# A mixture-of-experts loop: dispatch products moved behind the bias products, combine split into two passes inside the next pair

## The chip, the cores and the metric

The program runs on one core of one Trainium2 chip. The metric is the device time of one execution in microseconds (us); the median of three runs of the kernel before is 2145.57 us (2145.54 to 2147.9). A core has TensorE (matrix products; PE in the profile, its weight loads PEld), VectorE (DVE), ScalarE (ACT), GpSimd (POOL) and SyncE (SP), which issues the transfers from HBM here, carried out by 16 DMA engines.

## The reference

A small network on 256 tokens of width 1024: two mixing layers with cross attention and feed-forward, and then one block with a hybrid mixer and a mixture of experts. Only the last part, the experts, is touched by the change:

```python
logits = ht @ w_router + b_router
top_val, top_idx = lax.top_k(logits, 4)          # 32 experts, 4 for each token
gates = jax.nn.softmax(top_val, axis=-1)
...
hg = xblk @ w_gu[e] + b_gu[e]                    # 1024 x 2048, float32
x_glu, x_lin = hg[:, :1024], hg[:, 1024:]
act = min(x_glu, 7) * sigmoid(1.702 * min(x_glu, 7)) * (clip(x_lin, -7, 7) + 1)
y = act @ w_down[e] + b_down[e]                  # 1024 x 1024, float32
out[token] += gate * y
```

All weights are float32 and each is used once: an expert has (1024 x 2048 + 1024 x 1024) x 4 bytes = 12.6 MB, the 32 experts 403 MB.

## The kernel before

Experts are worked in 16 pairs (numbered 0 to 15 here, `moe`, L2107). A pair shares one tile of 128 token slots: pair 0 has 64 slots for each expert; the other pairs, ordered by load, have 96 for a busy expert and 32 for a light one. For each pair the program makes:

1. **dispatch** (`dispatch`, L2115): VectorE builds a selection matrix `Dm` (L2121, in a tile of the pool `sl`), TensorE multiplies the token rows by it (`dx`, 16 products of 128x128), and `modulate` (L2006) scales and shifts the result into `xg` on ScalarE and VectorE. There is one `xg`, so this comes when the pair before has read it.
2. **gate and up** (`gu`): for each k of 8, 16 products of 512 columns. A product of a 32-slot part uses a 32-column strip of TensorE's array, and four parts lie beside each other; three strips belong to the busy expert, one to the light one. Each needs its expert's 1 MB weight tile for this k. Then the bias products (L2194, bfloat16).
3. **swiglu** (L2313): on VectorE, ScalarE, VectorE, VectorE, in tiles `sg` and `sl`, two of each; then transposes on TensorE (`at`, L2209) and a copy to `ya` (L2210).
4. **down** (`dn`, L2223): 64 products of 512 columns with eight 1 MB tiles of weights.
5. **gate matrix**: VectorE builds `gw` (L2232), TensorE transposes it, ScalarE copies it to `GT` (L2235).
6. **combine** (`cb`, L2250): four float32 products of 512 columns scatter the pair's `y` to token rows; VectorE adds them to `acc` (L2251).

In the source the next pair's dispatch stands behind down (`DP = 2`). The order on each engine is written by the tile framework's scheduler, from its own estimate of when operands are ready; so in pairs 1 to 5 the 16 `dx` products follow the last `dn` product, and in later pairs they lie between `dn` products. Each engine works its queue in order.

Weights go through a ring of buffers of 22 MB, in 1 MB tiles (L1908 to L1936): the pools `blk` and `fb`, and six tiles `ringp` taken in turn (`ringt`, L1953). SP issues a transfer when the buffer's last reader is done. In pair 6 `overflow_table` (L2323) also takes one tile from `ringt`, as scratch for VectorE.

The last pair is different: `last_down` (L2254) works down in three column blocks, each followed by its combine, and the closing norm.

Of the kernel before, what the change touches and what calls it, by code (L numbers as in the profile page):

```python
# [47 lines left out]
SGB, SLB = 2, 2  # L48
# [14 lines left out]
D = 1024  # L63
T = 256
DFF = 2752
NFB = 22
NE = 32
# [158 lines left out]
class Net:  # L226
# [1880 lines left out]
    def moe(self):  # L2107


        nc = self.nc  # L2110
# [1 line left out]
        Wg, Wd = self.dr["w_gu_2"][0], self.dr["w_down_2"][0]  # L2112
        xg, pre = self.xg, self.pre

        def dispatch(pos, es, caps, first=False):  # L2115

            offs = (0, caps[0])
            Dm = self.mt2("sl", [128, 512], bufs=SLB)[:, 0:256].rearrange("p (t s) -> p t s", t=2)
            for tt in range(2):
                for i in range(2):  # L2120
                    nc.vector.tensor_scalar(Dm[:, tt, offs[i]:offs[i] + caps[i]], slot[:, 0:caps[i]], pos[:, tt, es[i]:es[i] + 1],  # L2121
                                            self.rs[:, tt:tt + 1], op0=OP.is_equal, op1=OP.mult)

            nb = 4 if first else 2
            w = 8 // nb
            dps = [self.ps("dx").rearrange("p (k t) -> p k t", k=4) for _ in range(nb)]
            for db, tt in [(db, tt) for tt in range(2) for db in range(8)] if first else [(db, tt) for db in range(8) for tt in range(2)]:

                self.mm(dps[db // w][:, db % w, :], self.x[tt][:, db * 128:db * 128 + 128], Dm[:, tt, :],
                        start=(tt == 0 and (not first or db % w == 0)), stop=(tt == 1))  # L2130
                if db % w == w - 1 and tt == 1:
                    self.modulate(xg, dps[db // w], db // w, w)

        for pair in range(NE // 2):
            first, last = pair == 0, pair == NE // 2 - 1
            if first:
                gate, pos = self.gate, self.posm
# [19 lines left out]
            def wd(i, u):  # L2157
                if first:
                    return Wd[e[i], 256 * u:256 * u + 256, :].rearrange("(a p) c -> p a c", p=128)
                if last and u < 2:  # L2160
                    return Wd[bass.ds(e[i], 1), 512 * u:512 * u + 512, 0:512].rearrange("b (a p) c -> p (b a) c", p=128)
                if last:
                    return Wd[bass.ds(e[i], 1), :, 256 * u:256 * u + 256].rearrange("b (a p) c -> p (b a) c", p=128)
                return Wd[bass.ds(e[i], 1), 256 * u:256 * u + 256, :].rearrange("b (a p) c -> p (b a) c", p=128)

            if first:
                dispatch(pos, es, caps, True)
# [24 lines left out]
            for n in range(4):  # L2192
                for o, m, i in parts:
                    self.mm(pg[n][o:o + m], sel[0:96, es[i]:es[i] + 1].to_broadcast([96, m]),  # L2194
                            self.b3[0:96, 512 * n:512 * n + 512], start=False)
            nxt = lambda at: dispatch(self.posp, (2 + pair, NE - 1 - pair), (96, 32)) if at == DP and pair < NE // 2 - 1 else None
            nxt(0)
            if last:

                self.pa = [self.ps("cb")[:, 0:256] for _ in range(2)]  # L2200
                for tt in range(2):
                    self.mm(self.pa[tt], self.ident, self.acc[tt][:, 768:1024], stop=False)
                self.warm("last")
            aT = self.ya().rearrange("p (k s) -> p k s", k=8)
            for n in range(2):
                act = self.swiglu(pg[n], pg[n + 2])
                pt = self.ps("at").rearrange("p (f s) -> p f s", f=4)
                for f in range(4):
                    nc.tensor.transpose(pt[:, f, :], act[:, 128 * f:128 * f + 128], self.ident)  # L2209
                nc.scalar.mul(aT[:, 4 * n:4 * n + 4, :], pt, 1.0 / 1.702)  # L2210
            nxt(1)
            pd = [self.ps("dn") for _ in range(2)] if not last else None
            if last:
                ws = [self.ring_pair([wd(i, u) for i in range(2)]) for u in range(4)]
            else:
                ws = [[self.ring(wd(i, u)) for i in range(2)] for u in range(4)]
            for u, w in enumerate(ws if not last else ()):
                for a in range(2):
                    k = 2 * u + a
                    for n in range(2):  # L2220
                        for o, m, i in parts:
                            c0 = a * 1024 + 512 * n
                            self.mm(pd[n][o:o + m], aT[:, k, o:o + m], w[i](c0), start=(k == 0), stop=(k == 7))  # L2223
            nxt(2)

            pgt = self.ps("gw")
            for tt in range(2):
                gw = self.mt2("gw", [128, 192])[:, 0:128]
                for i in range(2):
                    q = slice(es[i], es[i] + 1)  # L2230
                    with self.later():
                        nc.vector.tensor_scalar(gw[:, offs[i]:offs[i] + caps[i]], slot[:, 0:caps[i]], pos[:, tt, q], gate[:, tt, q], op0=OP.is_equal, op1=OP.mult)  # L2232
                nc.tensor.transpose(pgt[:, tt * 128:tt * 128 + 128], gw, self.ident)
            GT = self.mt2("GT", [128, T])
            nc.scalar.copy(GT, pgt[:, 0:T])  # L2235
            if pair == 6:
                self.overflow_table()
            elif pair == 8:
                self.overflow_slots()
            if last:  # L2240
                self.last_down(ws, aT, parts, GT)
                break
# [3 lines left out]
            for tt in range(2):  # L2246
# [76 lines left out]
    def overflow_table(self):  # L2323
# [4 lines left out]
        with self.tc.issue_after(self.last_ring.ins):  # L2328
# [15 lines left out]
        nc.vector.tensor_tensor(oh, rk.unsqueeze(1).to_broadcast([32, 16, 96]),  # L2344
                                self.C2("iota16")[0:32].unsqueeze(2).to_broadcast([32, 16, 96]), op=OP.is_equal)
        eb = self.mt("ovid", [32, 3, 16])
        for x, row in enumerate((e3, self.C2("off")[0:32], self.C2("rid")[0:32])):
            nc.vector.tensor_tensor(t2, oh, row.unsqueeze(1).to_broadcast([32, 16, 96]), op=OP.mult)
            nc.vector.tensor_reduce(eb[:, x, :], t2, axis=AX.X, op=OP.add)
# [184 lines left out]
```

## Time and profile before

| | us |
|---|---|
| median of three runs | 2145.57 |
| the profiled execution | 2153.04 |
| its span, first to last instruction | 2150.9 |
| pairs of experts, from the first gate-and-up product of pair 0 | from 1149.8 to 2150.9 |

The profiled execution is one of the kernel before, 2.1 us longer than the span that its instructions cover, and 7.5 us above the median. Over the whole span TensorE is busy 94%, VectorE 44%, ScalarE 31%. That share mixes a first half with moderate traffic from HBM and the experts' half, in which about 410 GB/s are moved. A busy TensorE need not be a TensorE at its peak: the end of a product is modelled. A float32 product has two records in the trace, so `dn` has x128 for its 64 products, `dx` x32, and `cb` x8. So the stretches are read one by one, by the windows, the timeline and the waits of SP.

### The profile page before, as it was taken

To read this page: it belongs to the slowest core of one execution; us is meant where nothing else is said; L and a number is where in the kernel's file an instruction comes from. 1 tells how busy PE (TensorE), PEld (TensorE's weight loads), DVE (VectorE), ACT (ScalarE), POOL (GpSimd) and SP (SyncE) were. 2 spreads that over 40 slices of the span, in tenths; PEclk is the share of its full clock that TensorE was granted. 3 is DMA by queue.
4 is the path that set the end of the run, shared out by engine and by line. 5 is a ranking of instruction groups with operands and counts; after the bars stand their busy time and mean duration, and the time that the engine had idled before them with its cause. 6 is when DMAs were issued, how large, how long until landed. Compare 5 with 4: busy or idle time off the path is not lost.

```text
span 2150.9 us, 37883 instructions
## 1 busy us (share of the span) xinstructions
PE 2015.1 (94%) x15056; PEld 1286.3 (60%) x15056; DVE 937.9 (44%) x1854; ACT 670.9 (31%) x1331; POOL 74.7 (3%) x97
## 2 busy tenths in 40 slices
PE   7999999999997899998989999999999999999997
PEld 6876798999985789997874333333233333333332
DVE  6764655777766457778554111111141111111122
ACT  6523554555654355555333100000000100000011
POOL 1200000000000000002001000000000000000000
PEclk9999999999998899999989999999999999999999
DMA  7459454666634546665858999999899999999992
GB/s 210 147 190 289 126 171 128 192 190 181 184 108 118 166 137 187 182 187 159 310 193 298 376 412 412 412 412 412 359 354 409 409 410 409 410 411 411 407 386 91
DMA packets 327765, 589.14 MB, mean 274 GB/s; under 512 B 25778, under 2 KB 216626, under 8 KB 318242
## 3 DMA queue, kind: packets, MB, share of 16 engines
q1 hardware_dynamic: 327586, 586.70, 76.7%
q8 instruction: 119, 1.95, 0.4%
q14 instruction: 60, 0.49, 0.1%
HBM read 585.58 MB, written 1.05 MB: 273 GB/s over the span
## 4 chain that ended last, share of the span: by engine, by line
PE 87%; DVE 4%; ACT 2%; issue 1%; DMA 1%; POOL 1%; ACTq 0%; SPq 0%; DVEq 0%; POOLq 0%
PE gu L362 22%; PE dn L362 13%; PE ug L362 11%; PE acc L362 9%; PE pj L362 6%; PE mk L362 4%; PE cb L362 3%; PE dx L362 3%; PE qp L362 2%; PE ada L362 1%; PE po L362 1%; PE tm L362 1%; PE accd L362 1%; PE at L2209 1%; DMA raw<-in_w_ada_dram 1%
## 5 line engine op out<-in xcount | busy, mean ns | idle before, releaser
L388 DVE TENSOR_TENSOR lo<-raw,hi 128x512 fp32r<-128x512 f32 x578 | 378.7, 695 | 162.2 <-ACT hi L387 146.8
L387 ACT CAST hi<-raw 128x512 fp32r<-128x512 f32 x578 | 328.7, 618 | 325.4 <-issue 85.0
L362 PE MATMUL gu<-Bring,xg 128*32 128x512 f32 (+1 forms) x3000 | 373.0, 594 | 0.0
L362 PEld LDWEIGHTS gu<-Bring,xg 128*32 128x32 f32 (+1 forms) x3000 | 110.9, 111 | 239.1 <-issue 219.3
L362 PE MATMUL dn<-Bring,ya 128*32 128x512 f32 (+2 forms) x1688 | 231.3, 599 | 1.3
L2317 DVE TENSOR_SCALAR sg<-gu 128x512 f32<-128x512 f32 x32 | 20.6, 686 | 433.1 <-PE gu L362 433.1
L362 PE MATMUL ug<-Bxh,hi 128*128 128x256 f32 x688 | 193.9, 282 | 1.4 <-ACT Bxh L487 1.4
L362 PE MATMUL ug<-Bxl,hi 128*128 128x256 f32 x688 | 193.7, 282 | 0.3 <-DVE Bxl L488 0.3
L362 PE MATMUL ug<-Bxh,lo 128*128 128x256 f32 x688 | 193.6, 282 | 0.0
L2318 ACT ACTIVATE sg<-sg 128x512 f32<-128x512 f32 x32 | 19.7, 629 | 506.6 <-DVE sg L2317 506.6
L362 PE MATMUL gu<-ring,xg 128*32 128x512 f32 (+1 forms) x968 | 174.2, 596 | 0.0
L362 PE MATMUL pj<-Bxh,hi 128*128 128x256 f32 x472 | 140.4, 298 | 8.6 <-ACT hi L387 4.1
L362 PE MATMUL pj<-Bxh,lo 128*128 128x256 f32 x472 | 138.0, 294 | 2.4 <-DVE lo L388 2.4
L362 PE MATMUL pj<-Bxl,hi 128*128 128x256 f32 x472 | 137.4, 292 | 0.9 <-DVE Bxl L488 0.6
L362 PEld LDWEIGHTS dn<-Bring,ya 128*32 128x32 f32 (+1 forms) x1688 | 60.7, 113 | 125.7 <-issue 112.5
L362 PEld LDWEIGHTS ug<-Bxh,hi 128*128 128x128 f32 x688 | 129.8, 189 | 3.9 <-ACT Bxh L487 1.8
L362 PEld LDWEIGHTS ug<-Bxl,hi 128*128 128x128 f32 x688 | 130.2, 189 | 1.9 <-DVE Bxl L488 0.5
L362 PEld LDWEIGHTS ug<-Bxh,lo 128*128 128x128 f32 x688 | 130.1, 189 | 0.0
L362 PEld LDWEIGHTS pj<-Bxh,hi 128*128 128x128 f32 x472 | 93.0, 197 | 13.5 <-ACT hi L387 5.3
L362 PEld LDWEIGHTS pj<-Bxh,lo 128*128 128x128 f32 x472 | 92.5, 196 | 5.2 <-DVE lo L388 3.0
L362 PEld LDWEIGHTS pj<-Bxl,hi 128*128 128x128 f32 x472 | 92.9, 197 | 3.8 <-issue 1.8
L362 PEld LDWEIGHTS gu<-ring,xg 128*32 128x32 f32 (+1 forms) x968 | 47.3, 111 | 75.9 <-issue 73.4
(725 smaller groups left out, 3141.5 us busy)
## 6 DMA issues: line engine op xcount, KB each, us to landing
Bring<-in_w_gu_dram SPq DMA_DIRECT2D x366, 512.0 KB, 10.2
Bring<-in_w_down_dram SPq DMA_DIRECT2D x198, 512.0 KB, 10.8
ring<-in_w_gu_dram SPq DMA_DIRECT2D x73, 1024.0 KB, 12.5
raw<-in_ffn_w_up_dram SPq DMA_DIRECT2D x84, 512.0 KB, 4.2
ring<-in_w_down_dram SPq DMA_DIRECT2D x29, 1024.0 KB, 13.3
raw<-in_w_ada_dram SPq DMA_DIRECT2D x48, 512.0 KB, 5.0
raw<-in_ffn_w_down_dram SPq DMA_DIRECT2D x42, 512.0 KB, 3.6
raw<-in_xattn_wkv_dram SPq DMA_DIRECT2D x32, 512.0 KB, 4.0
```

Of the source, the lines that this page charges most:

```text
L362: return self.nc.tensor.matmul(out, lhsT, rhs, start=start, stop=stop, skip_group_check=True)
L387: nc.scalar.copy(hi[:, s], raw[:, s])
L388: nc.vector.tensor_tensor(lo[:, s], raw[:, s], hi[:, s].bitcast(F32), op=OP.subtract)
L2209: nc.tensor.transpose(pt[:, f, :], act[:, 128 * f:128 * f + 128], self.ident)
L2317: nc.vector.tensor_scalar(g, pglu, 7.0, None, op0=OP.min)
L2318: nc.scalar.activation(g, g, AF.Silu, scale=1.702)
```

## The change

The parts of the diff that matter; the function `selection` is the first half of the old `dispatch`.

```diff
-DP = 2
+CB = 1
...
-        def dispatch(pos, es, caps, first=False):
+        def selection(pos, es, caps):
             offs = (0, caps[0])
             Dm = self.mt2("sl", [128, 512], bufs=SLB)[:, 0:256].rearrange("p (t s) -> p t s", t=2)
...
+            return Dm
+
+        def dispatch(Dm, first=False):
...
+        pending = None
...
                             self.mm(pg[n][o:o + m], xg[:, k, o:o + m], w[i](512 * n), start=(k == 0), stop=False)
+                if k == CB and pending:
+                    pending()
...
-                nc.tensor.transpose(pgt[:, tt * 128:tt * 128 + 128], gw, self.ident)
-            GT = self.mt2("GT", [128, T])
-            nc.scalar.copy(GT, pgt[:, 0:T])
+                with self.tc.issue_after(biased.ins):
+                    nc.tensor.transpose(pgt[:, tt * 128:tt * 128 + 128], gw, self.ident)
...
+                GT, gs = self.mt2("GT", [128, T], F32R), self.mt2("gs", [128, 1])
+                nc.vector.tensor_scalar(GT, pgt[:, 0:T], 0.0, None, op0=OP.is_gt)
+                nc.scalar.activation(self.mt2("gw", [128, 192]).bitcast(BF16)[:, 0:T], pgt[:, 0:T], AF.Identity, accum_out=gs)
+                with self.later():
+                    Dm = selection(self.posp, (2 + pair, NE - 1 - pair), (96, 32))
+            acts = [self.swiglu(pg[n], pg[n + 2]) for n in range(2)]
+            if not last:
+
+                with self.tc.issue_after(biased.ins):
+                    dispatch(Dm)
...
-            y = self.ya()
-            nc.scalar.copy(y[:, 0:512], pd[0])
-            nc.vector.tensor_copy(y[:, 512:1024], pd[1])
-            for tt in range(2):
+
+            yh, yl = self.mt2("ya", [128, D], F32R, bufs=1), []
+            for n in range(2):
+                h, t = yh[:, 512 * n:512 * n + 512], self.mt2("sl", [128, 512], F32R, bufs=SLB)
+                nc.scalar.mul(h, pd[n], gs)
+                nc.vector.scalar_tensor_tensor(t, pd[n], gs, h.bitcast(F32), op0=OP.mult, op1=OP.subtract)
+                yl.append(t)
+
+            def pending(GT=GT, yh=yh, yl=yl):
                 for n in range(2):
                     s = slice(512 * n, 512 * n + 512)
-                    p = self.ps("cb")
-                    self.mm(p, GT[:, tt * 128:tt * 128 + 128], y[:, s])
-                    nc.vector.tensor_tensor(self.acc[tt][:, s], p, self.acc[tt][:, s], op=OP.add)
-            nxt(3)
+                    for tt in range(2):
+                        p = self.ps("cb")
+                        g = GT[:, tt * 128:tt * 128 + 128]
+                        self.mm(p, g, yh[:, s], stop=False)
+                        self.mm(p, g, yl[n], start=False)
+                        nc.vector.tensor_tensor(self.acc[tt][:, s], p, self.acc[tt][:, s], op=OP.add)
...
-        oh, t2 = (t[0:32, 0:1536].rearrange("p (a b) -> p a b", a=16)
-                  for t in self.ringt().bitcast(BF16).rearrange("p (x c) -> x p c", x=2))
...
+        oh, t2 = (self.mt2("sg", [128, 512], bufs=SGB).bitcast(BF16)[0:32, 0:768].rearrange("p (a b) -> p a b", a=8) for _ in range(2))
+        for b in (slice(0, 8), slice(8, 16)):
```

In words: the dispatch products of the next pair and the two transposes of the gate matrix now stand behind the bias products, while swiglu runs. `GT` becomes a matrix of zeros and ones, the gate of each slot a column `gs`; down's result is multiplied by `gs` when it leaves PSUM, as a high part (ScalarE) and the rest (VectorE), both in the format `fp32r` that TensorE multiplies in one pass. The combine has two such products in place of each float32 one, and is written behind the gate-and-up products of k = 1 of the next pair. The table of pair 6 uses two `sg` tiles, in two halves, in place of a ring tile. Pair 15 keeps its gate matrix, float32 combine and `last_down`. SP's order of weight transfers is the same in both kernels.

TensorE's queue behind the bias products of pair 4 (`b` bias, `sel3p` selector) in the kernel before:

```order
L362 MATMUL gu_13626<-b_12166,sel3p 32x512
L2209 MATMUL at_13830<-c_70,sg_13824 128x128 x4
L2209 MATMUL at_13842<-c_70,sg_13836 128x128 x4
L362 MATMUL dn_13848<-Bring_13850,ya_13823 32x512 x3
...
L362 MATMUL dn_13849<-Bring_13879,ya_13823 32x512
L362 MATMUL dx_13951<-sl_13946,h_66 128x128
L362 MATMUL dx_13951<-sl_13946,h_68 128x128
```

And in the kernel after, at the same place:

```order
L362 MATMUL gu_13654<-b_12166,sel3p 32x512
L2212 MATMUL gw_13867<-c_70,gw_13868 128x128
L2212 MATMUL gw_13867<-c_70,gw_13872 128x128
L362 MATMUL dx_13898<-sl_13881,h_66 128x128
L362 MATMUL dx_13898<-sl_13881,h_68 128x128
...
L2237 MATMUL at_13925<-c_70,sg_13886 128x128 x4
L2237 MATMUL at_13931<-c_70,sg_13892 128x128 x4
L362 MATMUL dn_13937<-Bring_13939,ya_13924 32x512 x3
```

The two gate transposes and all 16 dispatch products (`dx`) moved from behind `dn` to ahead of the swiglu transposes (`at`).

TensorE's queue near the start of pair 9's gate and up (k = 1; `x3` the busy expert's three strips, the single rows the light expert's) in the kernel before:

```order
L362 MATMUL gu_15666<-Bring_15694,xg 32x512 x3
L362 MATMUL gu_15667<-Bring_15694,xg 32x512 x3
L362 MATMUL gu_15668<-Bring_15695,xg 32x512 x3
L362 MATMUL gu_15669<-Bring_15695,xg 32x512 x3
L362 MATMUL gu_15666<-ring_15698,xg 32x512
L362 MATMUL gu_15667<-ring_15698,xg 32x512
L362 MATMUL gu_15668<-ring_15698,xg 32x512
L362 MATMUL gu_15669<-ring_15698,xg 32x512
```

And in the kernel after (k = 0), where the combine of pair 8 stands between the two experts' products of one k:

```order
L362 MATMUL gu_15759<-Bring_15762,xg 32x512 x3
L362 MATMUL gu_15760<-Bring_15762,xg 32x512 x3
L362 MATMUL cb_15807<-ya_15730,GT_15555 128x512
L362 MATMUL cb_15811<-ya_15730,GT_15555 128x512
L362 MATMUL cb_15807<-sl_15731,GT_15555 128x512
L362 MATMUL cb_15811<-sl_15731,GT_15555 128x512
...
L362 MATMUL gu_15757<-Bring_15765,xg 32x512
L362 MATMUL gu_15758<-Bring_15765,xg 32x512
```

The eight `cb` products moved into the next pair, behind the busy expert's products of its first k; in both kernels the light expert's four follow the other's twelve, in the kernel after from pair 4 on and in part of pair 3, before from pair 7 on.

VectorE's queue in swiglu of pair 5 in the kernel after:

```order
L2337 TENSOR_SCALAR sg_14297<-gu_14062 128x512
L2337 TENSOR_SCALAR sg_14303<-gu_14063 128x512
L2339 TENSOR_SCALAR sl_14298<-gu_14064 128x512
L2224 TENSOR_SCALAR GT_14287<-gw_14278 128x256
L2340 SCALAR_TENSOR_TENSOR sg_14297<-sl_14298,sg_14297 128x512
L2339 TENSOR_SCALAR sl_14304<-gu_14065 128x512
L2340 SCALAR_TENSOR_TENSOR sg_14303<-sl_14304,sg_14303 128x512
```

Ahead of the second `sl` there is now the first product of swiglu: `Dm` holds one of the two `sl` tiles until the last `dx` product has read it. In the kernel before both `sl` come first.

## Rows read from the trace of the kernel before

**Rows 1.** The page, parts 1 and 2: TensorE; GB/s in 40 slices of the span

```profile
PE 2015.1 (94%) x15056; PEld 1286.3 (60%) x15056; DVE 937.9 (44%) x1854; ACT 670.9 (31%) x1331; POOL 74.7 (3%) x97
...
GB/s 210 147 190 289 126 171 128 192 190 181 184 108 118 166 137 187 182 187 159 310 193 298 376 412 412 412 412 412 359 354 409 409 410 409 410 411 411 407 386 91
```

**Rows 2.** Windows of 20 us (stretch, its length, engines busy, PEclk, DMA share, GB/s)

```profile
1160.00:1180.00 20.00, 20.00 (x90) 6.58 (x87) 4.71 (x10) 1.06 (x3) 0.00 (x0) 1.00 0.99 369
...
1220.00:1240.00 20.00, 20.00 (x192) 5.98 (x184) 0.00 (x0) 0.00 (x0) 0.00 (x0) 1.00 0.96 355
...
1540.00:1560.00 20.00, 17.32 (x149) 5.55 (x144) 4.73 (x11) 2.37 (x4) 0.00 (x0) 0.91 0.64 258
1560.00:1580.00 20.00, 17.54 (x106) 8.19 (x104) 11.62 (x21) 2.46 (x6) 0.00 (x0) 0.91 0.73 272
...
2040.00:2060.00 20.00, 17.47 (x118) 6.15 (x110) 4.58 (x10) 2.42 (x4) 0.00 (x0) 0.91 0.92 358
...
2080.00:2100.00 20.00, 20.00 (x139) 7.99 (x141) 2.77 (x4) 1.17 (x2) 0.00 (x0) 1.00 1.05 384
2100.00:2120.00 20.00, 18.34 (x164) 5.83 (x156) 3.13 (x6) 1.23 (x2) 0.00 (x0) 1.00 0.44 139
```

**Rows 3.** Timeline of pair 4 and the next (start, us, engine, line, what, [idle before])

```profile
1422.98 1.05 PE L362 MATMUL gu<-b,sel3p 96*32 96x512 bf16 x16
...
1425.82 1.28 DVE L2320 SCALAR_TENSOR_TENSOR sg<-sl,sg 128x512 f32<-128x512 f32 x2
...
1426.56 1.36 PE L2209 MATMUL at<-c,sg 128*128 128x128 f32 x8 [2.53 <-DVE sg L2320]
...
1427.96 15.41 PE L362 MATMUL dn<-Bring,ya 128*32 128x512 f32 x128
...
1443.31 3.84 PE L362 MATMUL dx<-sl,h 128*128 128x128 f32 x32
...
1449.15 0.69 PE L2233 MATMUL gw<-c,gw 128*128 128x128 f32 x2 [2.00 <-DVE gw L2232]
...
1450.29 5.40 PE L362 MATMUL cb<-ya,GT 128*128 128x512 f32 x8 [0.46 <-ACT GT L2235]
...
1483.11 1.05 PE L362 MATMUL gu<-b,sel3p 96*32 96x512 bf16 x16
```

**Rows 4.** Timeline of TensorE, pair 9's gate and up products

```profile
1696.88 5.40 PE L362 MATMUL cb<-ya,GT 128*128 128x512 f32 x8
...
1732.33 0.60 PE L362 MATMUL gu<-b,sel3p 96*32 96x512 bf16 x2
```

**Rows 5.** Timeline of TensorE at the end: the last pair, bias and down products

```profile
2115.55 0.64 PE L362 MATMUL gu<-b,sel3p 96*32 96x512 bf16 x8
...
2121.51 7.50 PE L362 MATMUL dn<-Bring,ya 128*32 128x512 f32 x70
...
2137.73 1.93 PE L362 MATMUL dn<-Bring,ya 128*32 128x256 f32 x32
```

**Rows 6.** SP's own waits (us, count, longest) and its transfers, 1525 to 1600 us

```profile
SPq L1935 <- PE dn L362: 18.6, 1, 18.6
...
1564.67 0.33 SPq L1935 DMA_DIRECT2D ring<-in_w_gu_dram  x1
```

**Rows 7.** VectorE, pair 6: the table's first and last large operations (timeline)

```profile
1572.05 1.75 DVE L2344 TENSOR_TENSOR ring<-sl,ct 32x1536 bf16<-32x1536 f32 x1
...
1585.43 1.74 DVE L2349 TENSOR_REDUCE ovid<-ring 32x16 f32<-32x1536 bf16 x1
```

**Rows 8.** Timeline of TensorE, pair 2's down products

```profile
1309.25 1.26 PE L2209 MATMUL at<-c,sg 128*128 128x128 f32 x8 [2.53 <-DVE sg L2320]
...
1324.52 3.84 PE L362 MATMUL dx<-sl,h 128*128 128x128 f32 x32
```

**Rows 9.** Timeline of TensorE: products of 256 columns in one pass

```profile
705.48 0.28 PE L362 MATMUL qp<-Bxl,hi 128*128 128x256 f32 x1
705.60 0.28 PE L362 MATMUL qp<-Bxh,lo 128*128 128x256 f32 x1
```

More of the change, by code (lines that the diff above doesn't have):

```diff
@@ L2166, in moe @@
             if first:
-                dispatch(pos, es, caps, True)
+                dispatch(selection(pos, es, caps), True)
             pg = [self.ps("gu") for _ in range(4)]
@@ L2193, in moe @@
                 for o, m, i in parts:
[L2194 to L2200, printed above, removed]
-                for tt in range(2):
[L2202 to L2224, printed above, removed]
+                    biased = self.mm(pg[n][o:o + m], sel[0:96, es[i]:es[i] + 1].to_broadcast([96, m]),
+                                     self.b3[0:96, 512 * n:512 * n + 512], start=False)
             pgt = self.ps("gw")
@@ L2232, in moe @@
                         nc.vector.tensor_scalar(gw[:, offs[i]:offs[i] + caps[i]], slot[:, 0:caps[i]], pos[:, tt, q], gate[:, tt, q], op0=OP.is_equal, op1=OP.mult)
-                nc.tensor.transpose(pgt[:, tt * 128:tt * 128 + 128], gw, self.ident)
-            GT = self.mt2("GT", [128, T])
-            nc.scalar.copy(GT, pgt[:, 0:T])
+                with self.tc.issue_after(biased.ins):
+                    nc.tensor.transpose(pgt[:, tt * 128:tt * 128 + 128], gw, self.ident)
+            if last:
+                GT = self.mt2("GT", [128, T])
+                nc.scalar.copy(GT, pgt[:, 0:T])
+                self.pa = [self.ps("cb")[:, 0:256] for _ in range(2)]
+                for tt in range(2):
+                    self.mm(self.pa[tt], self.ident, self.acc[tt][:, 768:1024], stop=False)
+                self.warm("last")
+            else:
+                GT, gs = self.mt2("GT", [128, T], F32R), self.mt2("gs", [128, 1])
[3 more added lines that the diff above has]
+                    Dm = selection(self.posp, (2 + pair, NE - 1 - pair), (96, 32))
@@ new lines, in moe @@
+            acts = [self.swiglu(pg[n], pg[n + 2]) for n in range(2)]
+            if not last:
+                with self.tc.issue_after(biased.ins):
+                    dispatch(Dm)
+            aT = self.ya().rearrange("p (k s) -> p k s", k=8)
+            for n in range(2):
+                pt = self.ps("at").rearrange("p (f s) -> p f s", f=4)
+                for f in range(4):
+                    nc.tensor.transpose(pt[:, f, :], acts[n][:, 128 * f:128 * f + 128], self.ident)
+                nc.scalar.mul(aT[:, 4 * n:4 * n + 4, :], pt, 1.0 / 1.702)
@@ new lines, in moe @@
+            if last:
+                ws = [self.ring_pair([wd(i, u) for i in range(2)]) for u in range(4)]
+                self.last_down(ws, aT, parts, GT)
+                break
+            pd = [self.ps("dn") for _ in range(2)]
+            ws = [[self.ring(wd(i, u)) for i in range(2)] for u in range(4)]
+            for u, w in enumerate(ws):
+                for a in range(2):
+                    k = 2 * u + a
+                    for n in range(2):
+                        for o, m, i in parts:
+                            c0 = a * 1024 + 512 * n
+                            self.mm(pd[n][o:o + m], aT[:, k, o:o + m], w[i](c0), start=(k == 0), stop=(k == 7))
@@ L2239, in moe @@
                 self.overflow_slots()
-            if last:
-                self.last_down(ws, aT, parts, GT)
-                break
-            y = self.ya()
-            nc.scalar.copy(y[:, 0:512], pd[0])
-            nc.vector.tensor_copy(y[:, 512:1024], pd[1])
-            for tt in range(2):
+            yh, yl = self.mt2("ya", [128, D], F32R, bufs=1), []
+            for n in range(2):
+                h, t = yh[:, 512 * n:512 * n + 512], self.mt2("sl", [128, 512], F32R, bufs=SLB)
[3 more added lines that the diff above has]
+            def pending(GT=GT, yh=yh, yl=yl):
                 for n in range(2):
                     s = slice(512 * n, 512 * n + 512)
-                    p = self.ps("cb")
-                    self.mm(p, GT[:, tt * 128:tt * 128 + 128], y[:, s])
-                    nc.vector.tensor_tensor(self.acc[tt][:, s], p, self.acc[tt][:, s], op=OP.add)
-            nxt(3)
+                    for tt in range(2):
+                        p = self.ps("cb")
[3 more added lines that the diff above has]
+                        nc.vector.tensor_tensor(self.acc[tt][:, s], p, self.acc[tt][:, s], op=OP.add)
     def last_down(self, ws, aT, parts, GT):
@@ L2340, in overflow_table @@
         nc.vector.tensor_copy(v3(e3), self.erow[0:32].unsqueeze(1).to_broadcast([32, 3, NE]))
-        oh, t2 = (t[0:32, 0:1536].rearrange("p (a b) -> p a b", a=16)
-                  for t in self.ringt().bitcast(BF16).rearrange("p (x c) -> x p c", x=2))
-        nc.vector.tensor_tensor(oh, rk.unsqueeze(1).to_broadcast([32, 16, 96]),
-                                self.C2("iota16")[0:32].unsqueeze(2).to_broadcast([32, 16, 96]), op=OP.is_equal)
         eb = self.mt("ovid", [32, 3, 16])
-        for x, row in enumerate((e3, self.C2("off")[0:32], self.C2("rid")[0:32])):
-            nc.vector.tensor_tensor(t2, oh, row.unsqueeze(1).to_broadcast([32, 16, 96]), op=OP.mult)
-            nc.vector.tensor_reduce(eb[:, x, :], t2, axis=AX.X, op=OP.add)
+        oh, t2 = (self.mt2("sg", [128, 512], bufs=SGB).bitcast(BF16)[0:32, 0:768].rearrange("p (a b) -> p a b", a=8) for _ in range(2))
+        for b in (slice(0, 8), slice(8, 16)):
+            nc.vector.tensor_tensor(oh, rk.unsqueeze(1).to_broadcast([32, 8, 96]),
+                                    self.C2("iota16")[0:32, b].unsqueeze(2).to_broadcast([32, 8, 96]), op=OP.is_equal)
+            for x, row in enumerate((e3, self.C2("off")[0:32], self.C2("rid")[0:32])):
+                nc.vector.tensor_tensor(t2, oh, row.unsqueeze(1).to_broadcast([32, 8, 96]), op=OP.mult)
+                nc.vector.tensor_reduce(eb[:, x, b], t2, axis=AX.X, op=OP.add)
         nc.vector.tensor_copy(ci[:, 0:16], eb[:, 0, :])
```

## The prediction

> **What bounds the kernel now.** I read the page's slices first, then the windows of the experts' half, then the waits of SP where a window is low, then the timeline of single pairs and of the end. The page shows two halves: up to the 21st slice traffic is moderate, and from the 23rd on it stands at 407 to 412 GB/s in nearly every slice [rows 1]. The reader is to see a flat ceiling with one notch (359 and 354). In the windows the DMA share is about 1 wherever the rate is about 410, so the 16 DMA engines are full [rows 2]. TensorE is busy 94% of the span in the same profile [rows 1]. So two resources are near their limits, and which one ends last has to be read pair by pair.
>
> A pair of experts is 25.2 MB (two times 12.6), 61.4 us at 410 GB/s. TensorE took 60.1 us from the bias products of pair 4 to those of pair 5 [rows 3], and from pair 4 to pair 9 (1732.33) it kept to 61.9 us a pair [rows 3, 4]. Neither waits much for the other: TensorE sits 22 MB of ring behind the transfers. It shows at the end: in the window from 2100 us 139 GB/s remain, 2.8 MB, so at full rate the last weights are there at 2106.8 [rows 2]; the last pair's down starts only at 2121.5 and the span ends at 2150.9 [rows 5]. The end is thus the transfers' end plus 44.1 us in which TensorE works off what it lags behind. The change can gain in two places: holes in the transfers, and that lag.
>
> **The holes.** The windows from 1540 to 1580 us have 258 and 272 GB/s [rows 2]: 20 x (1 - 258/410) + 20 x (1 - 272/410) = 14.1 us of transfer time lost. In the same stretch SP waits 18.6 us, once, in a `ringp` transfer for a down product, and issues at 1564.67 [rows 6]. That is pair 6: its table takes one turn of the six `ringp` tiles, so the next weight tile falls on a buffer whose down product of pair 6 is still to come. The window from 2040 loses 2.5 us and that from 2080 loses 1.3 us, both with SP behind TensorE; the four from 1160 to 1240, of which the first and the last are shown, lose 6.3 us [rows 2].
>
> **The change part by part.**
>
> *The table.* It no longer takes a ring tile; the wait of 18.6 us has no cause left, and 14.1 us of transfers come back. VectorE has 14 operations on half the columns in place of 7 of 1.74 us, so 12.2 us again, beside pair 7's gate and up of 27 us; without that cover TensorE would wait up to 12 us once, still under its lag [rows 7]. Bounds: 0 to 14.1; I take 14.1.
>
> *Dispatch behind the bias.* In pair 4 TensorE idles 2.53 us ahead of the swiglu transposes, runs 3.84 us of `dx` behind down, idles 2.00 us for `gw`, has 0.69 us of gate transposes and 0.46 us of idle for `GT` [rows 3]. After, `gw` and `dx` (0.7 + 3.84) run while VectorE and ScalarE do swiglu. The new `GT` (VectorE) and gate sum (ScalarE) lie beside `dx`; the moved step issues no transfer, and SP's order stays. What is late next is the second `sl`, which waits for the last `dx` product since `Dm` holds its buffer: 0.64 us for `sl`, 0.64 us for the product with `sg` (half of the pair of 1.28), then half of the transposes of 1.26, about 2.0 us from the end of `dx` to the start of down [rows 3, 8]. Queued behind that `sl` on VectorE are the second product and four `modulate` operations, which the next gate and up needs only 14 us later. Bounds of this gap: 0.6 (transposes alone) to 3.9 us (the old path from the first idle to down: 2.53 + 1.36).
>
> *Clock.* Windows in which such an idle falls (1540, 2040) have a mean granted clock of 0.91, so TensorE is at 1.2 GHz for part of them [rows 2]; in pair 4 down took 15.4 us against 14.0 in pair 2, where the transposes ended at 1310.5 and `dx` began at 1324.5 [rows 3, 8]. The combine took 5.4 us for four float32 products. With no idle ahead I take the 14.0.
>
> *Combine.* Eight one-pass products of 512 columns: the rows with 256 columns follow each other by 0.12 us at full clock, so 0.24 us each and 1.9 us in all [rows 9]; bounds 1.9 to 3.8 (the lower clock level). Two multiplications on ScalarE and two subtractions on VectorE (about 0.65 us each, by the 128x512 rows) come ahead, some 2 us, hidden by the first 3.4 us of the next gate and up. But all strips of the array are needed for `cb`, and it stands between the busy expert's twelve products and the light expert's four of one k. These four then have nothing beside them: a sixteenth of 14.0 us each, 3.5 us more. Bounds 0 to 3.5, I take 3.5.
>
> *Order of the two experts.* From pair 4 on the light expert's products stand in fours behind the other's twelve. The kernel before has that in pair 9: from the combine's end at 1702.3 to the last bias product at 1732.9 it took 30.6 us; pair 5, in the other order, took 27.4 us from 1455.7 to its first bias product, plus 1.05 [rows 3, 4]. So the light strip works beside the others, one k later, and the order costs about 2 us. The Trainium skill, "TensorE: Matmul & The Clock Gate", section "The mechanism" of Part 3, lets products of different strips overlap but calls them "strict FIFO, no reordering" in start and end. By that rule the light expert's four would start one after another behind the twelve, the gate and up would be 42 us and the pair 69; by the row they are 29.4 (without bias) and 56.4. The trace disagrees with the rule at pair 9's 30.6 us.
>
> *Sum for TensorE.* 27.4 gate and up + 2 order + 3.5 + 1.9 combine + 1.05 bias + 0.7 + 3.84 + 2.0 + 14.0 down = 56.4 us, against 60.1 in pair 5's period and 61.4 for the transfers. TensorE becomes the faster by 5 us a pair. Over the 14 pairs from 1 to 14 that is 70 us, more than the lag of 44, so in the last third it waits for weights.
>
> *Pair 0.* Its down now stands behind a dispatch (3.84 + about 2 us later), and pair 1 starts about 5 us earlier, since the dispatch, `gw` and combine that followed are gone. SP's `ringp` transfers wait for the first and its other transfers for the second. Bounds -5 to +5 us for the transfers; I take 0 and leave the 6.3 us.
>
> *The end.* Transfers end at 2106.8 - 14.1 - 2.5 - 1.3 = 2088.9. Behind them: the last pair's down weights are 8.4 MB, 20.5 us, so its gate and up can end 20.5 - 3.4 = 17.1 us before the last landing (3.4 us is one k), swiglu takes about 5, the first down block 6.9 (half of 14.0), the second 3.4, its combine 1.7: they end at about the last landing. Then 3.4 us for the third block, and from the end of the third block at 2139.7 to 2150.9 before, 11.2 us [rows 5]: 14.6. A TensorE that waits for weights may run at 1.2 GHz here, up to 15 us more for 15 us of products. I take 18, near the low end, as the lower level cost 1.4 us in pair 4. The span: 2106.9, 44.0 less than 2150.9. The profiled execution is 7.5 us above the median; taken off the median it is 2145.6 - 44.0 = 2101.6.
>
> **The rivals.**
>
> *TensorE stays behind.* Only the holes close, as the lower clock or waits among the strips keep TensorE at 61 us a pair. For it: 60.1 and 15.4 us are what it does today [rows 3]. Against: the idles that cost it are gone. The end keeps its 44.1 us: 17.9 gained, 2127.7.
>
> *The hole in pair 6 comes back elsewhere*, since the table now holds both `sg` tiles and swiglu of pair 7 waits. For it: 12.2 us of VectorE work on one path. Against: 27 us to do it in. 14.1 us less gain: 2115.7.
>
> *Nothing*: the lag is refilled by pair 0 and the last pair at the lower clock, and the hole with it. Its time is 2145.6. Against: a TensorE that needs 56 us for what takes 61 to bring does not fall behind.
>
> *Slower: the strips block.* From pair 4 on, the light expert's four products of a k start only as the busy expert's twelve end, one after another. Then a k is six steps of 0.87 us (a sixteenth of 14.0): four of the busy expert's, with the light one's first product beside the last of them, two more of the light one's alone, and its last beside the first of the next k. Eight k are 42 us in place of 29.4, the pair 69. (The rule of the skill above would have it so.) It decides from 62.9 us a pair: from pair 4's bias at 1423.0 to the last pair's at 2115.5 were 11 pairs of that mean [rows 3, 5]. Eleven pairs at 69 are 67 us more, less about 15 gained in pairs 0 to 3 and 10 at the end: 2188. For it: the order of the rows now stands in eleven pairs and not eight. Against: pair 9's 30.6 us [rows 4].
>
> **How the numbers follow.** The forecast has 0.68, TensorE behind 0.16, the hole elsewhere 0.07, nothing 0.04, slower 0.05. A measurement of this kernel can tell about 0.2% from no change, 4 us. Faster is then 0.68 + 0.16 + 0.07 = 0.91, same 0.04, slower 0.05. The forecast's own range is 2091 (no loss in pair 0, 14.6 us at the end, and part of the first holes closed) to 2114 (12 us more at the end). The range reaches up to the first two rivals: 2091 to 2131.
>
> **What would show it.** Right: `dx` directly behind the bias products with no idle of 2.53 us ahead of `at`; no wait of SP near 18 us in pair 6 and about 410 GB/s through it; TensorE waiting for landings in gate and up of the later pairs; last weights at about 2089 and 18 us behind them. Wrong: a gate and up over 35 us without a wait for a landing (the strips), a new wait of SP for TensorE, or an end that still lies 40 us behind the last landing. The forecast fails as a whole if transfers rise or fall from 410 GB/s, since it is a sum over bytes.

## The result, and the profile after

The kernel after took 2117.89 us (median of 4 runs, 2112.25 to 2120.33), the kernel before 2146.74 us beside it: a ratio of 0.9848, 95% interval 0.9825 to 0.9871. Run again beside later experiments it took 2111.69 us (2108.74 to 2115.44), ratio 0.9817 (0.9789 to 0.9846). The forecast, 2101.6 us, is 0.9795 of the 2145.57 us it started from: faster, as forecast, inside the range of 2091 to 2131, but 10 to 16 us above the single value. One execution of the kernel before, in a later group, took 6055 us; it is in none of the ratios.

The page, against [rows 1]: TensorE's busy time, GB/s in 40 slices, and the shares of the chain that ended last.

```profile
PE 2029.5 (96%) x15056; PEld 1308.7 (62%) x15056; DVE 953.5 (45%) x1891; ACT 682.5 (32%) x1361; POOL 74.8 (4%) x97
...
GB/s 213 140 186 284 119 180 129 189 187 181 193 121 97 180 119 188 185 182 138 319 188 240 354 411 411 411 410 411 411 411 403 409 406 407 409 410 408 410 410 267
...
PE 71%; DMA 19%; DVE 2%; ACT 2%; issue 1%; POOL 1%; SPq 0%; ACTq 0%; DVEq 0%; POOLq 0%
```

The notch of 359 and 354 is gone. The same chain in the kernel before:

```profile
PE 87%; DVE 4%; ACT 2%; issue 1%; DMA 1%; POOL 1%; ACTq 0%; SPq 0%; DVEq 0%; POOLq 0%
```

The end was held by TensorE alone; now a fifth of the chain is transfers. Of these 410 us, 386 lie in the experts' half, where the chain of the kernel before has none. The chain around pair 10, and where its last transfer stands (start, us, what):

```profile
1727.94 11.31 DMA Bring<-in_w_gu_dram
1739.37 10.76 DMA Bring<-in_w_gu_dram
...
2062.83 13.32 DMA ring<-in_w_gu_dram
...
2076.20 6.47 PE gu L362 x46
```

The last transfer that TensorE waits for is thus a gate-and-up tile of the last pair, landed at 2076.15, 41.9 us before the end of the span (2118.0). The last pair's down weights land later, but nothing waits for them.

Windows of the kernel after, columns as in [rows 2]:

```profile
1200.00:1220.00 20.00, 19.75 (x119) 7.53 (x121) 3.67 (x10) 3.22 (x7) 0.00 (x0) 1.00 0.70 278
...
1540.00:1560.00 20.00, 20.00 (x137) 6.35 (x132) 14.75 (x24) 1.27 (x2) 0.00 (x0) 1.00 1.02 414
1560.00:1580.00 20.00, 20.00 (x155) 6.43 (x148) 4.33 (x10) 0.00 (x0) 0.00 (x0) 1.00 1.03 410
2040.00:2060.00 20.00, 20.00 (x153) 7.37 (x155) 3.89 (x6) 1.85 (x3) 0.00 (x0) 1.00 1.02 416
...
2080.00:2100.00 20.00, 18.96 (x172) 7.34 (x170) 7.14 (x11) 4.17 (x9) 0.00 (x0) 1.00 1.00 342
```

The stretch at 1540 is full (258 and 272 GB/s before) and at a clock of 1.00 (0.91 before); that at 2040 is full too (358 before). A new hole stands at 1200: 278 GB/s, which is 20 x (1 - 278/410) = 6.4 us. At 2080 the DMA engines are busy all the time (share 1.00) and yet move only 342 GB/s.

The granted clock over most of the experts' half, 1200 to 2100 us, in the kernel before and in the kernel after:

```profile
1200.00:2100.00 900.00, 841.76 (x6528) 304.74 (x6528) 164.62 (x356) 72.32 (x154) 0.00 (x0) 0.97 1.01 401
...
1200.00:2100.00 900.00, 890.85 (x6833) 336.07 (x6835) 185.90 (x399) 87.88 (x192) 0.00 (x0) 1.00 1.02 405
```

Before, TensorE was at its lower level for about 54 of these 900 us, in short stretches: two of them in pair 4, where the windows from 1427 to 1431 and from 1451 to 1455 have a mean of 0.57, right behind the idles of 2.53 and 2.00 us. After, it stayed at the upper level.

The swiglu of pair 2 in the kernel after, where TensorE still lags, against [rows 3]:

```profile
1295.44 1.05 PE L362 MATMUL gu<-b,sel3p 96*32 96x512 bf16 x16
...
1296.69 3.74 PE L362 MATMUL dx<-sl,h 128*128 128x128 f32 x32
...
1298.02 0.68 DVE L2340 SCALAR_TENSOR_TENSOR sg<-sl,sg 128x512 f32<-128x512 f32 x1
...
1298.73 0.69 DVE L2339 TENSOR_SCALAR sl<-gu 128x512 f32<-128x512 f32 x1
...
1300.27 1.04 PE L2237 MATMUL at<-c,sg 128*128 128x128 f32 x8
...
1301.61 0.63 PE L362 MATMUL dn<-Bring,ya 128*32 128x512 f32 x3 [0.31 <-ACT ya L2238]
```

The idles of 2.53, 2.00 and 0.46 us are gone; 0.31 us is left, for the copy to `ya`. The second `sl` starts at 1298.73, at the end of the first product (1298.02 + 0.68), and not after `dx` (behind which the transposes start at 1300.27): it takes the buffer of the first `sl`, not that of `Dm`.

Pair 9's gate and up, against [rows 4], with the last bias products, and one product of the combine; then the end, against [rows 5]:

```profile
1676.23 3.61 PE L362 MATMUL gu<-Bring,xg 128*32 128x512 f32 x24
...
1681.03 0.39 PE L362 MATMUL cb<-sl,GT 128*128 128x512 f32 x1
1681.26 0.39 PE L362 MATMUL cb<-ya,GT 128*128 128x512 f32 x1
...
1712.55 0.60 PE L362 MATMUL gu<-b,sel3p 96*32 96x512 bf16 x2
...
2087.74 7.50 PE L362 MATMUL dn<-Bring,ya 128*32 128x512 f32 x70
...
2102.76 3.64 PE L362 MATMUL dn<-Bring,ya 128*32 128x256 f32 x58
```

Gate and up of pair 9 lasts 36.9 us to the end of its last bias product (30.6 before), yet the kernel is faster: the order in fours and the combine between the fours are in it, and little of a wait (34.6 us in a run below in which TensorE waits for no landing). One product of the combine follows another by 0.23 us.

SP's waits for down products in the kernel after, 1480 to 1640 us (pair 6 and its neighbours), against [rows 6] (sum, count, longest):

```profile
SPq L1935 <- PE dn L362: 0.6, 2, 0.3
```

It was 18.6 us in one wait. The same view from 1160 to 1240 us:

```profile
SPq L1935 <- PE dn L362: 15.4, 1, 15.4
```

This one waits for pair 0's down, which the moved dispatch delays (10.0 before), and is the hole at 1200.

### The profile page after: what moved, and what is told of

Read it like the earlier page. It is cut to its first block, busy times and chain, and to the rows that moved or that the text cites. A ratio compares the mean times of both kernels' runs of the same rounds, so it can differ in the third digit from the quotient of the medians.

```text
span 2118.0 us, 37992 instructions
## 1 busy us (share of the span) xinstructions
PE 2029.5 (96%) x15056; PEld 1308.7 (62%) x15056; DVE 953.5 (45%) x1891; ACT 682.5 (32%) x1361; POOL 74.8 (4%) x97
## 3 DMA queue, kind: packets, MB, share of 16 engines
HBM read 585.58 MB, written 1.05 MB: 277 GB/s over the span
## 4 chain that ended last, share of the span: by engine, by line
PE 71%; DMA 19%; DVE 2%; ACT 2%; issue 1%; POOL 1%; SPq 0%; ACTq 0%; DVEq 0%; POOLq 0%
PE gu L362 14%; PE ug L362 12%; PE acc L362 10%; DMA Bring<-in_w_gu_dram 8%; PE dn L362 8%; DMA ring<-in_w_gu_dram 6%; PE pj L362 6%; PE mk L362 4%; DMA Bring<-in_w_down_dram 4%; PE qp L362 2%; PE dx L362 2%; PE ada L362 1%; PE po L362 1%; PE tm L362 1%; PE accd L362 1%
## 5 line engine op out<-in xcount | busy, mean ns | idle before, releaser
L362 PE MATMUL gu<-Bring,xg 128*32 128x512 f32 (+1 forms) x3000 | 438.1, 595 | 0.0
L362 PEld LDWEIGHTS gu<-Bring,xg 128*32 128x32 f32 (+1 forms) x3000 | 127.0, 110 | 264.0 <-issue 215.1
L362 PE MATMUL dn<-Bring,ya 128*32 128x512 f32 (+2 forms) x1688 | 202.0, 577 | 4.1 <-ACT ya L2238 4.0
L362 PE MATMUL gu<-ring,xg 128*32 128x512 f32 (+1 forms) x968 | 198.1, 597 | 2.7 <-DMA ring<-in_w_gu_dram 2.2
L362 PEld LDWEIGHTS gu<-ring,xg 128*32 128x32 f32 (+1 forms) x968 | 53.8, 111 | 119.1 <-issue 102.8
L2261 DVE SCALAR_TENSOR_TENSOR sl<-dn,gs,ya 128x512 fp32r<-128x512 f32 x30 | 21.2, 746 | 211.1 <-ACT ya L2260 211.1
## 6 DMA issues: line engine op xcount, KB each, us to landing
ring<-in_w_gu_dram SPq DMA_DIRECT2D x73, 1024.0 KB, 12.6
```

The source lines that it names most:

```text
L362: return self.nc.tensor.matmul(out, lhsT, rhs, start=start, stop=stop, skip_group_check=True)
L2261: nc.vector.scalar_tensor_tensor(t, pd[n], gs, h.bitcast(F32), op0=OP.mult, op1=OP.subtract)
```

## The experiments

My theory after the result: TensorE alone set the end before; the moved dispatch makes it faster than the transfers; from pair 5 on the transfers set the pace. The rivals were that the table's hole, the combine, or the strips decide.

**Is the table a gain of its own?** Two runs, the change's table put alone into the kernel before, and the old table put back into the kernel after:

```diff
-        oh, t2 = (t[0:32, 0:1536] ... for t in self.ringt()...)
+        oh, t2 = (self.mt2("sg", [128, 512], bufs=SGB)... for _ in range(2))
```

> The kernel before with only the table of pair 6 moved from the ring tile to two `sg` tiles. Theory (TensorE sets the end of the kernel before, the hole costs nothing by itself): SP's wait of 18.6 us in pair 6 goes and the transfers land up to 14 us earlier, but no product of the kernel before starts less than 9 us behind the landing of its weights, so the time stays within 4 us of 2146. Rival (the hole is a term of its own, as the prediction's sum had it): 14.1 us less, 2132.

> The kernel after with the table of pair 6 back in a ring tile. Theory (the wait needs a TensorE that lags): down of pair 6 ends at 1547.3 in the kernel after, before the moment at which SP comes to the buffer (1546.1 before, some 5 us later after), so SP waits under 2 us and the time is that of the kernel after, 2114 to 2120. Rival (the ring tile alone makes the hole): 14.1 us of transfers are lost again on the path that sets the end, 2128 to 2134.

Measured: the table alone 0.999 (0.9973 to 1.0008), no change; the kernel after with the old table 0.9832 (0.9814 to 0.9849), the gain of the kernel after. The windows of the first show that the hole did close:

```profile
1540.00:1560.00 20.00, 18.39 (x147) 6.54 (x148) 3.75 (x10) 2.01 (x4) 0.00 (x0) 1.00 1.02 410
1560.00:1580.00 20.00, 17.54 (x136) 7.54 (x138) 16.77 (x30) 1.88 (x5) 0.00 (x0) 1.00 1.03 409
```

And SP's wait for `dn` in the second, from 1480 to 1640, with the ring tile in use as before:

```profile
SPq L1935 <- PE dn L362: 0.3, 1, 0.3
```

So 14 us of transfers came back in the first and were worth nothing, and in the second the hole was not there, ring tile or not. The 18.6 us are a ring tile and a TensorE that lags, and cost nothing while TensorE sets the end. The rival fell in both. Most of the 14 us did not even last: near the end of the first run, from 1990 to 2110 us, SP waits for a lagging down product again, 14.7 us at once (5.6 in the kernel before).

```profile
SPq L1931 <- PE dn L362: 15.3, 3, 14.7
```

**Which half pays?** The kernel after with the old combine behind down, and the kernel after with selection, dispatch and gate transposes behind down:

```diff
-            yh, yl = self.mt2("ya", ...) ... def pending(...)
+            y = self.ya()      # float32, four products, directly
```

> The kernel after with the float32 combine of the kernel before, directly behind down. Theory (either half of the change is enough to make TensorE faster than the transfers): a pair takes TensorE about 49.6 - 1.9 + 5.4 + 1.5 = 54.6 us, still under 61.4, the 42 us of lag at pair 1 are worked off in seven pairs, and the time is 2114 to 2122. Rival (the combine is the part that pays): half of the gain is lost, about 2132.

```diff
-                with self.tc.issue_after(biased.ins):
-                    dispatch(Dm)
...
+            dispatch(selection(...))      # behind down, then gw, GT, gs
```

> The kernel after with selection, dispatch and the gate transposes of pairs 0 to 14 written behind down again; the two-pass combine in the next pair stays. Theory (either half is enough): the idle of 2.5 us ahead of the swiglu transposes comes back, and the next gate and up waits some 2 us for `modulate`; a pair takes TensorE 55 to 58 us, the lag is worked off in 7 to 12 pairs, 2114 to 2126. Rival (the dispatch is the part that pays): TensorE stays at about 60 us a pair and behind the transfers, 2132 or more.

Measured: old combine 2113.3 us, 0.982 (0.9801 to 0.9839), the whole gain. Old dispatch 2163.07 us, 1.0053 (1.0038 to 1.0068): slower than before, so my theory fell for this half: the rival's side, and further out than it said. The first has TensorE at 52.0 us a pair in pairs 1 to 3 (49.6 in the kernel after), both under 61.4, so the combine's 2.4 us a pair are off the path. The dispatch is the part that pays. What it gives a pair can be read off: from pair 4's 60.1 us [rows 3] to the 52.0 of the first run, 4.7 us are the idles (2.53 + 2.00 + 0.46 less 0.31) and 3.2 us the clock (down 15.41 to 13.94, the float32 combine 5.40 to 3.70, the latter as in pair 7 of a run shown below). Down of pair 5 in the second:

```profile
1493.71 1.92 PE L362 MATMUL dn<-Bring,ya 128*32 128x512 f32 x12
1495.56 0.71 PE L362 MATMUL dx<-sl,h 128*128 128x128 f32 x4
1496.20 1.93 PE L362 MATMUL dn<-Bring,ya 128*32 128x512 f32 x16
1498.06 0.49 PE L362 MATMUL dx<-sl,h 128*128 128x128 f32 x2
1498.48 1.90 PE L362 MATMUL dn<-Bring,ya 128*32 128x512 f32 x4
1500.32 1.16 PE L362 MATMUL dx<-sl,h 128*128 128x128 f32 x8
```

Four records of `dn` (two products) take 1.90 us, as long as sixteen (1.93). They start 0.43 us apart, one after another on one strip; the sixteen lie four beside each other. A `dx` product needs all strips, so the two products of one strip that stand between two `dx` run alone. Down with the dispatch in it lasts 23.1 us in this pair; apart they take 13.9 and 3.8. As an estimate from the rows of the whole stage, 3.5 of the 5.4 us more are two extra steps of 1.74 us (an eighth of 13.9) in which strips stand empty, and 1.9 us lie at the twelve changes from one kind of product to the other.

**Is it the mix, then?** The kernel before, and the kernel with the old dispatch, each with one more edit: no dispatch product ahead of the last down product.

```diff
+            with self.tc.issue_after(downed.ins):     # downed: last dn product
                 dispatch(...)
```

> The kernel before with one edit: the dispatch products of each pair may not start before the last down product, so that none lies between down products in pairs 6 to 14. Theory (the mix of dispatch and down products is a cost of its own): pairs 7 to 14 fall from 62.9 us to the 60 of pairs 1 to 6, TensorE ends about 22 us earlier, 2124 to 2128. Rival (only the idles ahead of the swiglu transposes and the gate transposes cost): they remain, and the mix had hidden part of them, so no gain or a loss: 2146 to 2155.

> The kernel with the two-pass combine and the old dispatch, and now no dispatch product may start before the last down product. Theory (the mix of dispatch and down products made that kernel slow): its pairs 5 to 14 fall from 64 us to the 58.5 to 60 of its pairs 1 to 4, and it ends some 40 us earlier, 2118 to 2128; what is left to the kernel after is the filled idle ahead of the swiglu transposes. Rival (its pairs are slow for the gate transposes and the combine among the gate and up products): no more than half of that, 2140 or more.

Measured: the kernel before with this edit alone 2130.4 us, 0.9905 (0.9879 to 0.9931), 20 us gained; the other 2123.97 us, 0.9872 (0.9846 to 0.9898), 39 us less than the 2163.07 without it. Down of pair 7 in the kernel before, its first products, four records alone, and the last:

```profile
1610.05 1.92 PE L362 MATMUL dn<-Bring,ya 128*32 128x512 f32 x12
...
1614.82 1.90 PE L362 MATMUL dn<-Bring,ya 128*32 128x512 f32 x4
...
1629.50 3.66 PE L362 MATMUL dn<-ring,ya 128*32 128x512 f32 x32
```

The same pair in the first run (swiglu, first `dn`, `dx`, gate transposes, combine):

```profile
1607.75 1.26 PE L2209 MATMUL at<-c,sg 128*128 128x128 f32 x8 [1.76 <-DVE sg L2322]
1609.15 7.50 PE L362 MATMUL dn<-Bring,ya 128*32 128x512 f32 x67
...
1623.05 3.84 PE L362 MATMUL dx<-sl,h 128*128 128x128 f32 x32
...
1628.88 0.68 PE L2235 MATMUL gw<-c,gw 128*128 128x128 f32 x2 [2.00 <-DVE gw L2234]
1630.03 3.70 PE L362 MATMUL cb<-ya,GT 128*128 128x512 f32 x8 [0.46 <-ACT GT L2237]
```

Down and `dx` last 13.9 + 3.8 = 17.7 us (23.1 mixed), and this outweighs the idles of 2.00 and 0.46 us that come back. The rival fell. The clock is not the cause: its mean over the span is 0.964 here and 0.966 in the kernel before, 0.970 and 0.971 in the other two. From pair 7's bias products to pair 15's it takes 61.5 us a pair (63.9 before), not the 60 that I expected. About half of the gain of the change or somewhat more, 20 of 33 to 39 us, is thus had by the order alone. The rest goes with the filled idles: in both runs TensorE still ends last (no transfer of the experts' half in the chain; in the second, 588 of the 589 MB are in at 2091.5 and the span ends at 2123.7), and the second differs from the kernel after only in the place of selection, dispatch and gate transposes. Whether the two-pass combine and the table, which only the second has, add to it behind a dispatch in the old place is open: the two intervals overlap.

**How fast is TensorE when the transfers don't hold it?** The kernel after with a quarter of the down weights brought in pairs 1 to 14 and used four times; and the same with the busy expert's twelve products ahead of the light one's four in every k.

```diff
-            ws = [[self.ring(wd(i, u)) for i in range(2)] for u in range(4)]
+            ws = [[self.ring(wd(i, u)) for i in range(2)] for u in range(4 if first else 1)]
+            ws = ws if first else ws * 4
```

> The kernel after with less to bring: in pairs 1 to 14 only the first quarter of the down weights is transferred and stands in for the other three (the result is not the network's). A pair is then 18.9 MB, 46 us at 410 GB/s. Theory (TensorE needs 49.6 us a pair, as in pairs 1 to 3 of the kernel after, and the later pairs are paced by the transfers): TensorE sets the pace at 49.6 us, pair 15 starts at about 1911 and the end is near 1975. Rival (gate and up of pairs 5 to 14 takes 42 us because of the strips): 62 us a pair as before, 2115.

> As the run before with a quarter of the down weights (it stands in for the rest, so the result is not the network's), and in every pair from 1 on the source has the busy expert's twelve products of a k first and the light expert's four behind them. Theory (the light strip works beside the others one k later): the pair of 49.6 us grows by at most the 2.4 us that pair 9 of the kernel before took more, 50 to 52 us. The prediction's terms: 2 for the order and 3.5 for the combine between the twelve and the four, 55. Rival (strips block in that order): gate and up 42 us, the pair 62.

Measured: 1985.03 us and 2039.35 us. The first, a pair (bias, dispatch, down, next bias):

```profile
1439.59 1.05 PE L362 MATMUL gu<-b,sel3p 96*32 96x512 bf16 x16
...
1440.85 3.74 PE L362 MATMUL dx<-sl,h 128*128 128x128 f32 x32
...
1445.77 13.94 PE L362 MATMUL dn<-Bring,ya 128*32 128x512 f32 x128 [0.31 <-ACT ya L2238]
...
1489.17 1.05 PE L362 MATMUL gu<-b,sel3p 96*32 96x512 bf16 x16
```

49.6 us, as in ten of the fourteen pairs within 0.3. In the second it is 53.5 us (53.8 in the pair shown), more than the 50 to 52 I expected: gate and up is 33.8 in place of 29.8 us, from the start of its first weight product to the end of its last. The same rows of it:

```profile
1396.19 0.40 PE L362 MATMUL gu<-b,sel3p 96*32 96x512 bf16 x3
...
1404.34 13.94 PE L362 MATMUL dn<-Bring,ya 128*32 128x512 f32 x128 [0.59 <-ACT ya L2238]
...
1449.97 0.40 PE L362 MATMUL gu<-b,sel3p 96*32 96x512 bf16 x3
```

So the order of the strips costs 4 us a pair and not 12; with either order TensorE stays under 61.4. The end came 10 us later than my 1975: from pair 8's bias to pair 9's it took 55.6 us (`overflow_slots` lies there) and to pair 15's 53.9. One window, 1400 to 1600, of the first of the two:

```profile
1400.00:1600.00 200.00, 198.76 (x1806) 75.27 (x1802) 59.31 (x124) 22.23 (x48) 0.00 (x0) 1.00 0.97 376
```

And of the kernel after:

```profile
1400.00:1600.00 200.00, 198.16 (x1472) 76.01 (x1472) 55.10 (x114) 20.99 (x46) 0.00 (x0) 1.00 1.02 411
```

TensorE is "busy" 198 us in both, but has 1806 records of products in the one and 1472 in the other. The busy share doesn't show the waits for landings; the count does.

**Does the hole of pair 0 cost?** The kernel after with selection and dispatch of pair 0 in the old place, and the kernel after again:

```diff
-            if not last:
+            if not first and not last:
                 with self.tc.issue_after(biased.ins):
                     dispatch(Dm)
...
+            if first:                          # behind down
+                dispatch(selection(...))
```

> The kernel after, with only pair 0 in the old order: down of pair 0 ahead of the selection and dispatch of pair 1. Theory (the transfers set the end, so a hole in them costs its whole length): down of pair 0 starts some 5.5 us earlier, SP's wait of 15.4 us for it shrinks to about 10, the 6.6 us lost around 1200 shrink to about 1, and the time is 5 us under that of the kernel after measured beside it. Rival (a hole so early is absorbed, since TensorE lags 42 us there): same time.

> The kernel after unchanged, beside the others on one chip. Theory: 0.983 to 0.985 of the time before; ahead of the experts its transfers stand within 1.5 us of those of the kernel before, so that the 4.5 us by which its first profile was late there belong to that execution. Rival: the 4.5 us come back, and then they belong to the change.

Measured: 2110.5 us, 0.9804 (0.9775 to 0.9834), against 2111.69 us, 0.9817 (0.9789 to 0.9846): not told apart. SP's wait for pair 0's down, with pair 0 in the old order:

```profile
SPq L1935 <- PE dn L362: 11.3, 1, 11.3
```

Its window at 1200:

```profile
1200.00:1220.00 20.00, 20.00 (x140) 8.85 (x137) 3.73 (x11) 2.77 (x6) 0.00 (x0) 1.00 1.01 411
```

The wait in the kernel after again:

```profile
SPq L1935 <- PE dn L362: 15.0, 1, 15.0
```

And its window:

```profile
1200.00:1220.00 20.00, 20.00 (x125) 6.75 (x122) 1.86 (x3) 1.27 (x2) 0.00 (x0) 1.00 0.89 347
```

The hole closes, and the profiled span is 2109.9 against 2113.2 us although that execution was 3.7 us late ahead of the experts: 588 of the 589 MB are in at 2092.1 against 2095.7. The traces speak for 5 us or more, the times can't show it; it stays open. The first 150 MB are in at 878.9 us in the kernel before and in the kernel after again, at 883.4 in its first profile: those 4.5 us belong to that execution.

## Why the prediction was right, and where not

**What bounds the kernel: right.** TensorE set the end before (the table alone changed nothing), the transfers set the pace now, at the forecast rate of about 410 GB/s.

**The table, -14.1 us: the hole closed, the step failed.** It is no term of the table. With TensorE lagging it is worth 0 (0.999), with TensorE in step the ring tile makes no hole (0.983). I added it to the sum as if the edit brought it; it comes with the lag's end, so that the 14.1 us in the sum were right by luck.

**Dispatch behind the bias: right, and for more than I said.** It carries the gain. I priced the idles of 2.53 and 2.00 us and the clock (the full level in every pair, as I took it: 1.00 from 1200 to 2100 us); that it takes `dx` out from among the down products of pairs 6 to 14, 20 us over the program, I had only as "14.0 for down". The wait of the second `sl` for `dx` was wrong: 1.34 us from `dx` to down, not 2.0.

**Combine: cost right, worth nothing.** Eight times 0.23 = 1.8 us against 1.9. But the float32 one would have done as well (0.982).

**TensorE's sum, 56.4 us: 3 to 7 us too high.** It takes 53.5 with the strips in fours, which the sum has, and 49.6 in turns. Gate and up with the combine is 29.8, and I had 27.4 + 2 + 3.5 + 1.9 = 34.8; the order of the strips costs 4 us where I took 5.5, and pairs 1 and 2 don't have it. So the lag was gone at pair 5 and not in the last third: the periods are 49.6, 49.8, 54.1 us and then mostly 61 and more, and by the sum of bytes over time the bias products of pairs 1 to 4 come about 30, 18, 7 and 0 us behind the landing of their pair's gate-and-up weights (never under 12 in the kernel before; I had taken 42 at pair 1). That changed nothing in the end: beyond 61.4 a faster TensorE only waits. The rule of the Trainium skill that I weighed ("TensorE: Matmul & The Clock Gate", "The mechanism" of Part 3) would, by my reading, have made gate and up 42 us in the run with the twelve and four, and its pair 62; the 33.8 and 53.5 us say no.

**The transfers' end, -17.9 us: the term that was mis-sized.** In the kernel after again 588 MB are in at 2095.7 against 2108.3 before, -12.6. The 5.3 us that fail, by the same sum of bytes over time: pair 0, for which I took 0, loses 1.1 (4.3 at 230 MB, most of it given back by 260 MB, where the kernel before waited for pair 1); between 380 and 560 MB the lead falls from 13.1 to 10.9, as the page's slices there read 403 to 410 GB/s where before they read 407 to 411, whose cause I didn't find; and some 2 at 2080, where I had assumed 410 GB/s and the last pair's column blocks bring 342 with the DMA engines full. The 1.3 us that I read as a hole at 2080 before, with SP behind TensorE, were this too: the share there was 1.05 [rows 2].

**The tail: right as a sum, not as a path.** From 588 MB to the end of the span 42.6 us before, 2113.2 - 2095.7 = 17.5 after, -25.1 against the -26.1 forecast (44.1 to 18). But TensorE does not wait for these last bytes. The last landing that it waits for is the gate-and-up tile, some 41.9 us before the end in both profiles of the kernel after, with the old table and with pair 0 in the old order; with the old combine it is a down tile, 22.7 us before the end. So the 2 us at 2080 make the transfers' end later and the tail shorter by as much, and cost no time; that 17.5 meets 18 so closely is partly luck. The last down block took 3.64 us, about a quarter of 13.9, so the lower clock for which I had left 3.4 us cost nothing there.

**The basis.** Spans: 2150.9 to 2113.2, -37.7 against -44.0. I took this off a median of three; the kernel before gave medians of 2146.7 to 2153.5 in later groups of runs and single ones from 2142 to 2161. Of the 10 us between 2101.6 and 2111.69, 6.3 are the transfers' end and the tail together; the rest lies within that scatter.

## What to carry to other kernels

A hole in a saturated transfer queue is worth its length only if the engine behind the ring is not late itself; first ask who is last at the end, and how far the other lies behind. Products that need the whole array, put between products of single strips, make one strip's products run with the other strips empty: keep each kind together, and let the whole-array work fill the idle of another engine's stage. Judge a stage's speed by the products done in a stretch, not by the busy share.

## What was not expected of the hardware

Two down products of one strip (four records) between two whole-array products took 1.90 us, as long as eight over four strips (sixteen records, 1.93). Twelve then four in each k in place of turns cost 53.5 - 49.6 = 3.9 us a pair. The last pair's column blocks came at 342 GB/s with a DMA share of 1.00, against 410 for whole rows; their packets in the trace are of 2 and 1 KB, against 4 and 8 KB. In pair 4 of the kernel before the granted clock fell behind both idles of 2 us and more (0.57 over 4 us each), in pair 2 not behind the first (its down took 14.0 us [rows 8]); with the idles filled it stayed at 1.00 for 900 us.
